# Down projections by Strassen's method on quarters, and one shared ring of buffers, in a two-layer encoder trunk

## The chip, the core and the metric

The kernel runs on one core of one Trainium2 chip. The metric is device time in microseconds (us) of one execution. A core has a matrix engine (PE, with its weight loads shown apart as PEld), a vector engine (DVE), an activation engine (ACT), a general engine (POOL) and queues for transfers (SP's above all). Each engine works off its own instructions strictly in their order, and engines wait for one another at semaphores.

## The reference

Two layers of a Conformer-like block on 512 tokens of width 1024, all in float32:

```python
for l in range(DEPTH):
    x = x + 0.5 * swiglu(rms_norm(x, ffn1_norm[l]), ffn1_w_gate[l], ffn1_w_up[l], ffn1_w_down[l])
    h = rms_norm(x, mix_norm[l])
    p = h @ w_in[l]
    attn = mla_group(p[..., :o_kv], p[..., o_kv:o_pe], p[..., o_pe:o_cv], ...)
    conv = conv_group(p[..., o_cv:], conv_w[l], conv_b[l], conv_ln_g[l], conv_ln_b[l])
    x = x + jnp.concatenate([attn, conv], axis=-1) @ w_out[l]
    x = x + 0.5 * swiglu(rms_norm(x, ffn2_norm[l]), ffn2_w_gate[l], ffn2_w_up[l], ffn2_w_down[l])
    x = rms_norm(x, post_norm[l])

def swiglu(x, w_gate, w_up, w_down):
    return (jax.nn.silu(x @ w_gate) * (x @ w_up)) @ w_down
```

The feed-forward width is 2816. `mla_group` is attention with 8 heads, `conv_group` a causal depthwise convolution with 31 taps over 512 channels, then a layer norm and a silu.

## The kernel before

**Layout.** x is held transposed: 8 tiles of 128 features by 512 tokens. Every float32 product is made as three matmuls of a shorter float type: weights and activations are split into a high part `hi` (a cast on ACT) and a low part `lo` (source minus high part, on DVE), and `mm3` adds hi\*hi, hi\*lo and lo\*hi in PSUM. So each weight tile that comes in by a transfer costs a cast on ACT and a subtraction on DVE before PE may use it (`load_w`, `split_into`).

**A feed-forward half** (`ffn_body`; four in all) goes through 11 pairs of 128-wide column blocks in chunks of 2, 3, 3 and 3 pairs. Pairs of the first chunk make gate and up plainly while DVE and ACT prepare the operands `X` (`operands`). A later pair (`pair`) makes gate and up by Strassen's method in Winograd's form on quarters: four quarters a11, a12, a21, a22 of the weights come in, three sums of them and s3 are made on DVE, and seven products of 24 matmuls with 256 columns go into the PSUM banks bx, by and bz. After a chunk, each of the 8 output tiles m is a plain down projection: a weight tile is loaded and split, 6 x 3 matmuls of 512 columns run, and DVE adds the result into x (`order["evicted"]`).

**A mixing stage** (`mix_body`; two) makes the joint projection, latent queries and keys, then the attention of 8 heads as a software pipeline over stages (`turn`, `scores`, `turn_p`, `values`, `turn_out`; the last PE step of a head pair is the transposition in `turn_out`). The convolution runs beside it on other engines. Of its four tiles of channels, kind "D" runs on DVE; kind "A" (c = 1 and 2) makes each of 30 taps as a product `pr` on ACT (L765) and an addition into `y` on POOL (L769). Then POOL sums the four tiles (L783 to L785), PE makes their mean (L787), a layer norm follows, and the output projection uses the attention's four tiles first and the convolution's four afterwards.

**What sets the order.** The program is written in one order; a scheduler with a model of times then lists each engine's instructions. Tiles come from pools. A pool gives its buffers out in the order in which the program asks, and a tile that finds none free waits for an earlier one's last reader. `slot()` is such a pool, the ring: 41 tiles of 128 x 512. `tmp()` is another, of 5. `pr` has three buffers of its own, `y` two, `acc` two, `R` two.

## Time and profile before

| what | us |
|---|---|
| median of 3 runs (lowest, highest) | 1832.68 (1830.99, 1833.28) |
| the profiled execution's own time | 1831.62 |
| its span, first to last instruction | 1829.9 |
| PE busy | 1812.2 |
| DVE busy | 1357.7 |
| ACT busy | 938.6 |
| POOL busy | 333.2 |

Lines of the profile name the place (L769 is line 769 of the kernel), the engine, the operation, the tiles written and read with their numbers left out (`y<-y,pr`), and a shape. In the page's row of slices each digit is the busy share, in tenths, of one fortieth of the span. In a timeline a row has its start, its length, and in brackets the idle time of the engine before it with what ended that. Consecutive instructions of one engine overlap a little, so a row's length is more than the distance to the next start.

### The profile page before, as it was taken

What the parts mean: (1) busy time and instruction counts of PE and PEld (TensorE: products, weight loads), DVE (VectorE), ACT (ScalarE), POOL (GpSimd) and SP (SyncE); (2) the same over time, 40 slices, a digit from 0 to 9 for tenths busy, and PEclk for the clock granted to TensorE, in tenths of its full rate; (3) what the DMA queues carried; (4) which work ended last, traced back from release to release, by engine and by line L of the source; (5) the groups of instructions that cost most, each with busy time, mean ns of one, the idle gap of its engine ahead of it and who ended that gap; (6) DMA issues with size and microseconds to landing.
All of it is one profiled execution on the core that took longest, in us unless ns stands there. A gap on an engine that the chain in (4) does not pass through costs nothing.

```text
span 1829.9 us, 28080 instructions
## 1 busy us (share of the span) xinstructions
PE 1812.2 (99%) x11334; PEld 1625.6 (89%) x11334; DVE 1357.7 (74%) x1775; ACT 938.6 (51%) x1477; POOL 333.2 (18%) x239
## 2 busy tenths in 40 slices
PE   9999999999999999999999999999999999999998
PEld 7898989888788898989888999998878788989897
DVE  7976767589956985858769677675999669767674
ACT  5553535457953453535734535354679435535354
POOL 1000000248943000000310000002589410000001
PEclk9999999999999999999999999999999999999999
DMA  6242422324123142423512414123250322424122
GB/s 225 72 136 62 143 65 81 116 75 138 36 81 98 47 139 65 141 67 96 170 52 64 153 56 152 55 88 116 78 134 19 109 82 64 144 64 137 61 84 78
DMA packets 55426, 175.73 MB, mean 96 GB/s; under 512 B 6272, under 2 KB 6656, under 8 KB 55296
## 3 DMA queue, kind: packets, MB, share of 16 engines
q1 hardware_dynamic: 54000, 169.74, 29.4%
q0 software_dynamic: 1152, 4.19, 1.3%
q8 instruction: 88, 1.44, 0.3%
q14 instruction: 42, 0.34, 0.1%
q10 hardware_dynamic: 144, 0.00, 0.0%
HBM read 171.82 MB, written 2.10 MB: 95 GB/s over the span
## 4 chain that ended last, share of the span: by engine, by line
PE 85%; DVE 5%; ACT 4%; POOL 2%; issue 2%; DMA 1%; SPq 0%; ACTq 0%; POOLq 0%; DVEq 0%
PE ps L148 27%; PE ps L150 27%; PE ps L149 27%; PE ps L707 1%; ACT pr L765 1%; POOL y L769 1%; ACT r L679 1%; DVE wl L141 1%; DVE t L309 1%; DVE r L304 1%; PE ps L673 1%; PE ps L694 1%; DVE cv L761 1%; ACT wh L135 1%; PE ps L191 0%
## 5 line engine op out<-in xcount | busy, mean ns | idle before, releaser
L149 PE MATMUL ps<-r,wh 128*128 128x256 f32 (+1 forms) x3292 | 1060.8, 324 | 0.0
L150 PE MATMUL ps<-r,wl 128*128 128x256 f32 (+1 forms) x3292 | 1053.7, 324 | 2.7 <-DVE wl L141 1.4
L148 PE MATMUL ps<-r,wh 128*128 128x256 f32 (+1 forms) x3292 | 1053.6, 326 | 0.5 <-ACT r L154 0.3
L149 PEld LDWEIGHTS ps<-r,wh 128*128 128x128 f32 x3292 | 626.5, 190 | 51.5 <-issue 2.4
L148 PEld LDWEIGHTS ps<-r,wh 128*128 128x128 f32 x3292 | 622.3, 190 | 56.0 <-ACT wh L135 1.5
L150 PEld LDWEIGHTS ps<-r,wl 128*128 128x128 f32 x3292 | 622.9, 190 | 54.7 <-DVE wl L141 3.9
L237 ACT CAST wh<-fr 128x1024 fp32r<-128x1024 f32 x216 | 226.9, 1051 | 314.0 <-PE ps L149 227.9
L135 ACT CAST wh<-raw 128x768 fp32r<-128x768 f32 (+3 forms) x212 | 185.3, 880 | 331.1 <-PE ps L149 156.3
L239 DVE TENSOR_TENSOR wl<-fr,wh 128x1024 fp32r<-128x1024 f32 x216 | 264.2, 1223 | 75.7 <-ACT wh L237 72.7
L184 POOL TENSOR_TENSOR acc<-acc,t 128x512 f32<-128x512 f32 x45 | 77.8, 1738 | 1292.6 <-ACT t L180 1291.8
L141 DVE TENSOR_TENSOR wl<-raw,wh 128x768 fp32r<-128x768 f32 (+3 forms) x196 | 205.7, 1055 | 120.3 <-ACT wh L135 118.8
L433 DVE SCALAR_TENSOR_TENSOR x<-ps,x 128x512 f32<-128x512 f32 x126 | 86.8, 689 | 113.3 <-PE ps L150 113.3
L769 POOL TENSOR_TENSOR y<-y,pr 128x511 f32<-128x511 f32 (+14 forms) x120 | 157.0, 1309 | 54.0 <-ACT pr L765 46.5
L765 ACT ACTIVATE pr<-r,vec 128x511 f32<-128x511 f32 (+14 forms) x120 | 85.0, 729 | 12.7 <-POOL y L769 12.7
L761 DVE SCALAR_TENSOR_TENSOR cv<-r,vec,cv 128x511 f32<-128x511 f32 (+14 forms) x120 | 87.8, 732 | 3.4 <-ACT cv L757 2.1
L154 ACT CAST r<-t 128x512 fp32r<-128x512 f32 x96 | 55.8, 620 | 35.1 <-DVE t L282 22.2
L155 DVE TENSOR_TENSOR r<-t,r 128x512 fp32r<-128x512 f32 x96 | 64.8, 687 | 10.2 <-ACT r L154 10.2
L237 ACT CAST wh<-raw 128x1024 fp32r<-128x1024 f32 x36 | 37.7, 1048 | 66.7 <-PE ps L149 66.7
L239 DVE TENSOR_TENSOR wl<-raw,wh 128x1024 fp32r<-128x1024 f32 x36 | 44.1, 1226 | 28.4 <-ACT wh L237 28.3
L357 DVE TENSOR_TENSOR raw<-fr,fr 128x1024 f32<-128x1024 f32 x36 | 44.0, 1223 | 15.6 <-DMA fr<-in_wgu 15.6
L148 PE MATMUL ps<-wh,r 128*128 128x288 f32 (+2 forms) x144 | 48.5, 337 | 0.8 <-ACT r L652 0.8
L673 PE MATMUL ps<-r,r 96*128 96x384 f32 (+3 forms) x128 | 45.0, 462 | 2.6 <-ACT r L679 2.4
(189 smaller groups left out, 1627.2 us busy)
## 6 DMA issues: line engine op xcount, KB each, us to landing
fr<-in_wgu SPq DMA_DIRECT2D x144, 512.0 KB, 3.6
raw<-in_wd SPq DMA_DIRECT2D x96, 384.0 KB, 3.2
raw<-in_wgu SPq DMA_DIRECT2D x30, 512.0 KB, 3.6
raw<-in_wd SPq DMA_DIRECT2D x32, 256.0 KB, 2.7
raw<-in_wcv SPq DMA_DIRECT2D x16, 512.0 KB, 3.6
raw<-in_wout SPq DMA_DIRECT2D x16, 512.0 KB, 3.6
wl<-in_wout POOLq DMA_DIRECT2D x8, 512.0 KB, 6.9
raw<-in_wql SPq DMA_DIRECT2D x6, 512.0 KB, 3.6
```

The source lines that it names most:

```text
L135: order["cast"] = A.copy(hi[:, :w], raw[:, :w]).ins
L141: (G if kind in POOLW.split() else V).tensor_tensor(lo[:, :w], raw[:, :w], hi[:, :w].bitcast(FP), ALU.subtract)
L148: T.matmul(o, lh, rh, start=first, stop=False, skip_group_check=free)
L149: T.matmul(o, lh, rl, start=False, stop=False, skip_group_check=free)
L150: return T.matmul(o, ll, rh, start=False, stop=last, skip_group_check=free).ins
L184: (eng or (V if last else G)).tensor_tensor(self.acc, self.acc, sq, ALU.add)
L237: A.copy(hi[:, :w], src[:, :w])
L239: V.tensor_tensor(lo[:, :w], src[:, :w], hi[:, :w].bitcast(FP), ALU.subtract)
L433: order["evicted"] = V.scalar_tensor_tensor(x[:, m, :], pd, 0.5, x[:, m, :], ALU.mult, ALU.add).ins
L761: V.scalar_tensor_tensor(acc[:, s:], u[c][:, :S - s], tap(k), acc[:, s:], ALU.mult, ALU.add)
L765: A.activation(pr[:, s:], u[c][:, :S - s], AF.Copy, scale=tap(k))
L769: order["conv"] = G.tensor_tensor(acc[:, s:], acc[:, s:], pr[:, s:], ALU.add).ins
```

## The change

1. The down projections of chunks of three pairs (all but the last chunk of the last feed-forward half: eleven) go by Strassen's method too: `down` makes, for each half g of the output tiles, seven products of 18 matmuls with 256 columns from quarters of the down weights, and adds them into x from the banks px, py and pz after each product. px is not started anew between its products b11, t2, t1 and b22. `pair` makes the operands for it: combinations u and v of its two results s and s2, each split.
2. Two of a pair's seven low parts (a12 and a22) are made by `summed`: ACT writes the negated cast, and a transfer issued on POOL adds the source from memory onto it. Low parts have five buffers.
3. The ring has 49 tiles and now also serves `acc`, `R`, the latent keys `ck`, the accumulators `y` and the products `pr`. `tmp` has 6. The operands' even and odd halves use the quarters' buffers `fr`.
4. In the first feed-forward half the norm's first sums stand after half of a plain product more, and a pair's silu steps are written earlier.

```diff
-RING = 41
+RING = 49
+LOS = 5
...
-    tmps = ctx.enter_context(tc.tile_pool(name="tmps", bufs=5))
+    tmps = ctx.enter_context(tc.tile_pool(name="tmps", bufs=6))
-    rpool = ctx.enter_context(tc.tile_pool(name="rp", bufs=2))
...
+        def summed(p, q, src):
+            lo = low()
+            A.activation(lo, src, AF.Copy, scale=-1.0)
+            G.dma_start(out=lo, in_=wgu[l, p, q], accum_op=ALU.add)
+            hi = wpool.tile([P, WC], FR, tag="wh", name=nm("wh"))
+            A.copy(hi, src)
+            return hi, lo
...
-            product(by, split_into("a12", a12), "b21", True, True)
+            product(by, summed(p, 1, a12), "b21", True, True)
...
-            product(bz, split_into("a22", a22), "t4", False, True)
+            product(bz, summed(p, 3, a22), "t4", False, True)
...
-            return [split(s), split(s2)]
+            if not quartered:
+                return [split(s), split(s2)]
+            h0, h1 = slice(0, HS), slice(HS, S)
+            b = slot(FR)
+            A.copy(b[:, h0], s[:, h0])
+            V.tensor_tensor(b[:, h1], s[:, h0], b[:, h0].bitcast(FP), ALU.subtract)
+            b2 = split(s2)
+            u, v = tmp(), tmp()
+            V.tensor_tensor(u[:, h0], s[:, h1], s2[:, h1], ALU.subtract)
+            V.tensor_tensor(u[:, h1], u[:, h0], s[:, h0], ALU.subtract)
+            V.tensor_tensor(v[:, h0], s[:, h0], s[:, h1], ALU.subtract)
+            V.tensor_tensor(v[:, h1], s2[:, h0], u[:, h1], ALU.add)
+            us, vs = split(u), split(v)
...
+        def down(act, chunk):
+            n = 2 * NP * P
+            for g in range(2):
+                a11, a12, a21, a22 = (quarter() for _ in range(4))
+                for q, t in enumerate((a11, a12, a21, a22)):
+                    nc.sync.dma_start(out=t[:, :n], in_=wdq[l, g, chunk, q])
+                s3 = wpool.tile([P, WC], FP, tag="raw", name=nm("raw"), bufs=3)
+                px, py, pz = bank(), bank(), bank()
...
+                times(px, a11, "b11", True)
+                add(0, 0, px, 1)
+                times(py, a12, "b21", True)
+                add(0, 0, py, 1)
+                for o, u, v in ((s3, a11, a21), (a21, a21, a22), (a11, a11, a21), (a12, a12, a11)):
+                    V.tensor_tensor(o[:, :n], u[:, :n], v[:, :n], ALU.add)
+                times(px, a11, "t2", False)
+                add(1, 0, px, -1)
+                times(pz, s3, "t3", True)
+                add(1, 1, pz, 1)
+                times(px, a21, "t1", False)
+                add(1, 1, px, -1)
+                times(pz, a22, "t4", False)
+                add(1, 0, pz, 1)
...
+                times(px, a12, "b22", False)
+                add(0, 1, px, 1)
...
+            if p0 and not last:
+                down(act, (p0 - CHUNKS[0][1]) // NP)
+                continue
...
-                pr = kpool.tile([P, S], FP, tag="pr", name=nm("pr"), bufs=3)
+                pr = slot()
```

`times` splits the quarter (`split_into`) and issues the 18 matmuls; `add` is one DVE instruction that adds a bank, halved and signed, into two tiles of x.

**Where instructions moved.** The changed file is longer, so its lines have other numbers: the attention's exponentials are L679 before and L756 now, the casts L154 and L159, the convolution's products L765 and L842, its additions L769 and L846, the mean L787 and L864, low parts L239 and L244, additions into x L433 and L431.

ACT in the first layer's attention, before (`pr` products between the exponentials):

```order
L679 ACTIVATE r756_4489,sums753_4486<-ps751_4484,mx754_4487 128x384
L679 ACTIVATE r757_4490,sums753_4486<-ps752_4485,mx754_4487 128x512
L652 ACTIVATE r759_4512<-ps758_4507,gqs729_4409 96x512
L765 ACTIVATE pr946_5186<-r605_3766,vec_78 128x484
L679 ACTIVATE r766_4525,sums753_4486<-ps762_4521,mx765_4524 128x128
L765 ACTIVATE pr947_5189<-r605_3766,vec_78 128x483
L679 ACTIVATE r767_4526,sums753_4486<-ps763_4522,mx765_4524 128x384
L679 ACTIVATE r755_4488,sums753_4486<-ps750_4483,mx754_4487 128x256
```

and now, where its first convolution products stand (r987 is the cast of the last head pair's transposed output, r637 the accumulator of c = 1, r1002 and later the products):

```order
L774 COPY r977_5565<-ps976_5564 128x512
L159 CAST r982_5592<-ps981_5587 128x512
L159 CAST r987_5615<-ps986_5610 128x512
L834 ACTIVATE r637_4128<-r688_4338,vec_75 128x512
L842 ACTIVATE r1002_5681<-r688_4338,vec_75 128x511
L842 ACTIVATE r1003_5684<-r688_4338,vec_75 128x510
L842 ACTIVATE r1004_5687<-r688_4338,vec_75 128x509
```

All 60 products of the layer moved from among the attention's instructions to behind its last cast; the second layer is the same.

POOL in the same mixing stage, before (`rtok` is the norm's root, `acc` the sum of squares of the query latents, `y556` the accumulator of c = 1):

```order
L166 TENSOR_TENSOR rtok582_3651<-vtok580_3644,minus_half_98 128x4
L769 TENSOR_TENSOR y556_3558<-y556_3558,pr919_5105 128x511
L769 TENSOR_TENSOR y556_3558<-y556_3558,pr920_5108 128x510
L769 TENSOR_TENSOR y556_3558<-y556_3558,pr921_5111 128x509
L769 TENSOR_TENSOR y556_3558<-y556_3558,pr922_5114 128x508
L769 TENSOR_TENSOR y556_3558<-y556_3558,pr923_5117 128x507
L184 TENSOR_TENSOR acc616_3834<-acc616_3834,t619_3840 128x512
```

and now, the first additions, behind the four transfers for the output projection's weights:

```order
L141 DMA wl991_5623<-in_wout 128x1024
L141 DMA wl994_5630<-in_wout 128x1024
L141 DMA wl997_5637<-in_wout 128x1024
L141 DMA wl1000_5644<-in_wout 128x1024
L846 TENSOR_TENSOR r637_4128<-r637_4128,r1002_5681 128x511
L846 TENSOR_TENSOR r637_4128<-r637_4128,r1003_5684 128x510
L846 TENSOR_TENSOR r637_4128<-r637_4128,r1004_5687 128x509
```

Fifteen additions stood ahead of the keys' roots before, and the others among the transfers; now all 60 stand behind the transfers, and each reads a product from the ACT rows above.

DVE in the first down stage, before (around the 2nd and 3rd of the eight output tiles, `wl` being a low part):

```order
L433 SCALAR_TENSOR_TENSOR x_76<-ps254_1473,x_76 128x512
L141 TENSOR_TENSOR wl273_1582<-raw271_1578,wh272_1580 128x768
L433 SCALAR_TENSOR_TENSOR x_76<-ps258_1499,x_76 128x512
L141 TENSOR_TENSOR wl277_1608<-raw275_1604,wh276_1606 128x768
L357 TENSOR_TENSOR raw286_1663<-fr282_1655,fr284_1659 128x1024
```

and now (ps270 is px, ps271 py, ps272 pz; t259 is the last pair's u and r262 its low part, t260 is v; raw291 and fr289 are sums of the second half's quarters):

```order
L402 TENSOR_TENSOR t259_1475<-t242_1312,t253_1435 128x256
L404 TENSOR_TENSOR t260_1476<-t242_1312 128x256
L431 SCALAR_TENSOR_TENSOR x_73<-ps271_1499,x_73 128x2x256
L244 TENSOR_TENSOR wl284_1622<-fr268_1492,wh283_1620 128x768
L403 TENSOR_TENSOR t259_1475<-t259_1475,t242_1312 128x256
L437 TENSOR_TENSOR raw291_1674<-fr287_1666,fr289_1668 128x768
L405 TENSOR_TENSOR t260_1476<-t253_1435,t259_1475 128x256
L160 TENSOR_TENSOR r262_1482<-t259_1475,r261_1481 128x512
L160 TENSOR_TENSOR r264_1486<-t260_1476,r263_1485 128x512
L437 TENSOR_TENSOR fr289_1668<-fr289_1668,fr290_1669 128x768
L431 SCALAR_TENSOR_TENSOR x_73<-ps270_1498,x_73 128x2x256
L431 SCALAR_TENSOR_TENSOR x_73<-ps272_1500,x_73 128x2x256
```

The last pair's combinations and splits now stand between the first additions into x of the down stage, and PE's first t2 matmuls of that pair need r261 and r262. PE's own order has 12 matmuls of t3 and 12 of t2, those of the other two pairs, ahead of them.

More of the change, by code (lines that the diff above doesn't have):

```diff
@@ L214, in spread_sb @@
         ps = spread(r)
[L215 removed]
+        R = slot()
         A.copy(R, ps)
@@ L310, in diff @@
                 return t
-            for n in ("b11", "b21"):
-                for i in range(2):
-                    X[n].append(halved((es if n == "b11" else od)[i][:, :, 0:HS]))
+            for i in range(2):
+                e, o = wide(quarter()), wide(quarter())
+                for j in range(2):
+                    for par, t in ((0, e), (1, o)):
+                        m = 4 * i + 2 * j + par
+                        V.scalar_tensor_tensor(t[:, j], x[:, m, :], gain[:, m:m + 1], R, ALU.mult, ALU.mult)
+                        yield
+                b11, b12, b21, b22 = (v[:, :, h * HS:(h + 1) * HS] for v in (e, o) for h in range(2))
+                for n, src in (("b11", b11), ("b21", b21)):
+                    X[n].append(halved(src))
                     yield
-            for i in range(2):
-                b11, b12, b21, b22 = (v[i][:, :, h * HS:(h + 1) * HS] for v in (es, od) for h in range(2))
                 t3 = diff(b12, b22)
@@ new lines, in pair @@
+            V.tensor_tensor(b[:, h1], s[:, h0], b[:, h0].bitcast(FP), ALU.subtract)
[6 more added lines that the diff above has]
+            us, vs = split(u), split(v)
+            return [{"b11": (b[:, h0], b[:, h1]), "b21": [w[:, h0] for w in b2], "b22": [w[:, h1] for w in b2],
+                     "t3": [w[:, h0] for w in us], "t2": [w[:, h1] for w in us],
+                     "t1": [w[:, h0] for w in vs], "t4": [w[:, h1] for w in vs]}]
@@ L392, in ffn_body @@
             act = []
+            last = p1 == NF // 2 and halved < KD
             for p in range(p0, p1):
@@ L435, in ffn_body @@
                     done(m)
-            if last and halved < KD:
+            if last:
                 ms = range(halved, KD)
@@ L893, in encoder_kernel @@
     w0 = [tuple(wpool.tile([P, WC], t, tag=tag, name=nm(tag), bufs=n)
-                for t, tag, n in ((FP, "raw", 3), (FR, "wh", 4), (FR, "wl", 4))) for _ in range(2)]
+                for t, tag, n in ((FP, "raw", 3), (FR, "wh", 4), (FR, "wl", LOS))) for _ in range(2)]
     def half_w(q, gu):
```

103 lines of the change are left out of this document (61 added, 42 removed).

## Prediction

> **What bounds the kernel now.** I read the page first: the busy shares, the slices and the chain that ended last.
>
> ```profile
> PE 1812.2 (99%) x11334; PEld 1625.6 (89%) x11334; DVE 1357.7 (74%) x1775; ACT 938.6 (51%) x1477; POOL 333.2 (18%) x239
> PE   9999999999999999999999999999999999999998
> POOL 1000000248943000000310000002589410000001
> PE 85%; DVE 5%; ACT 4%; POOL 2%; issue 2%; DMA 1%; SPq 0%; ACTq 0%; POOLq 0%; DVEq 0%
> ```
>
> PE is never idle for long and makes up 85% of the chain: 1829.9 us is the sum of its matmuls. POOL works in earnest twice, in the two mixing stages. Next I asked for busy time by stage: one gate/up pair, one stage of eight down projections, one layer's attention, and what follows the attention (columns: stage, length, then busy time of PE, PEld, DVE, ACT, POOL).
>
> ```profile
> 268.94:289.13 20.19, 20.19 (x170) 20.16 (x169) 16.57 (x18) 11.56 (x16) 0.00 (x0) 1.00 0.34 105
> 329.40:362.20 32.80, 32.80 (x146) 27.19 (x145) 22.10 (x26) 16.69 (x24) 10.17 (x6) 1.00 0.41 128
> 451.50:516.50 65.00, 61.87 (x440) 50.78 (x439) 55.70 (x104) 58.13 (x133) 59.17 (x49) 1.00 0.23 51
> 516.50:530.40 13.90, 13.77 (x62) 10.44 (x60) 8.30 (x14) 6.38 (x11) 1.03 (x1) 1.00 0.00 0
> ```
>
> The FFN stages are PE alone. Attention keeps four engines near full at once, POOL at 59 of 65 us: it works off the convolution's additions beside the attention.
>
> **The products.** Busy times of matmuls overlap, so I take distances between starts from the timeline, six matmuls apart in each form.
>
> ```profile
> 299.79 0.28 PE L150 MATMUL ps<-r,wl 128*128 128x256 f32 x1
> 300.51 0.28 PE L150 MATMUL ps<-r,wl 128*128 128x256 f32 x1
> 327.80 0.39 PE L150 MATMUL ps<-r,wl 128*128 128x512 f32 x1
> 329.16 0.39 PE L150 MATMUL ps<-r,wl 128*128 128x512 f32 x1
> ```
>
> 0.120 us for 256 columns, 0.227 for 512: the half-width matmul costs 6% more per column. A chunk of three pairs had 8 x 6 x 3 = 144 of the wide form, 32.6 us; now it has 2 x 7 x 3 x 2 x 3 = 252 of the narrow one, 30.2 us. The eighth that Strassen's method saves shrinks to 2.4 us, and eleven chunks give **-26.4 us**.
>
> **What DVE gets in the chunk.** Prices, again by starts: 0.60 for an addition of 512 columns into x, 0.865 for a low part of 768, 0.34 for 256 columns, 1.13 for 1024.
>
> ```profile
> 337.63 0.69 DVE L433 SCALAR_TENSOR_TENSOR x<-ps,x 128x512 f32<-128x512 f32 x1
> 338.23 1.82 DVE L141 TENSOR_TENSOR wl<-raw,wh 128x768 fp32r<-128x768 f32 x2
> 339.96 1.79 DVE L161 SCALAR_TENSOR_TENSOR r<-x,vec,r 128x512 fp32r<-128x512 f32 x1
> 277.51 0.42 DVE L376 TENSOR_TENSOR t<-t,t 128x256 f32<-128x256 f32 x1
> 277.85 1.22 DVE L359 TENSOR_TENSOR fr<-fr,fr 128x1024 f32<-128x1024 f32 x1
> 278.98 1.22 DVE L239 TENSOR_TENSOR wl<-fr,wh 128x1024 fp32r<-128x1024 f32 x1
> ```
>
> In a pair two low parts leave DVE (-2.3) and four combinations, two splits and a narrower split come (+2.3): 16.6 of 20.2 us as before. In the down stage DVE had 8 x 0.865 + 8 x 0.60 = 11.7 us of its own; now it has 14 x 0.865 + 8 x 0.865 + 14 x 0.60 = 27.4 us against 30.2 of PE, and each sum in px is read by DVE before PE may continue in it, with one product of 18 x 0.12 = 2.16 us for cover. I walked DVE's queue from the end of the last pair's b22 product (time 0). PE has 10 matmuls of b11, 18 of b21, 12 each of t3 and t2 until 6.2, then needs the last pair's u split. Before that split DVE has a product of 256, the first addition (its sum is ready at 1.3), a low part, two combinations, the addition of b21, a low part, a combination, a sum of quarters and another combination: the split ends near 7.1, so PE waits 0.8. t1 waits for the addition of t2, behind a split and a sum of quarters: about 0.9. In the second half t1 waits about 0.4 in the same way. I take 2.0 per stage, **+22 us**; the bounds are 0 (DVE's 27.4 is below 30.2) and twice that, since the next pair's six instructions of 1.13 stand in the same queue.
>
> The two low parts made by a subtracting transfer cost ACT a copy each and POOL an issue each; POOL is idle there. One such transfer is in the trace:
>
> ```profile
> wl<-in_wout POOLq DMA_DIRECT2D x8, 512.0 KB, 6.9
> L138 ACT ACTIVATE wl<-raw 128x1024 fp32r<-128x1024 f32 x4 | 4.2, 1050 | 0.0
> L139 POOL DMA_DIRECT2D wl<-in_wout x8 | 7.5, 936 | 0.5 <-ACT wl L138 0.5
> ```
>
> The buffer of a12's low part comes free after the t3 product of the pair before. From there to its use are t1, t4, b22, a11 (4 x 2.88 = 11.5 us); it needs a copy behind t3 (a row of 0.58 for that size stands below), the negation of 1.05, the issue of 0.94 and 6.9 us, 9.5 together. Cost 0, with 2.0 us to spare; a transfer that lands later than that stops PE by the rest. In the first FFN half of a product now stands ahead of the first sums, which hides this wait: **-1.4**.
>
> ```profile
> 24.60 1.05 PE L191 MATMUL ps<-ones,acc 128*128 128x1 f32 x8 [1.42 <-DVE acc L184]
> ```
>
> The shared ring's first user is the mixing stage. Before, products `pr` had three buffers of their own, and both engines' orders show them between the attention's work. Now `pr` is a ring slot, asked for after all of the attention's slots; in the new order all 60 ACT products of a layer stand behind the attention's last cast, and all 60 POOL additions behind them. PE's order is unchanged: last turn of the attention, then the mean of the convolution (L787, now L864), and only behind it the output projection. What these took:
>
> ```profile
> 392.28 7.18 POOL L769 TENSOR_TENSOR y<-y,pr 128x511 f32<-128x511 f32 x5 [21.08 <-ACT pr L765]
> 476.34 35.47 POOL L769 TENSOR_TENSOR y<-y,pr 128x508 f32<-128x508 f32 x27 [1.12 <-ACT pr L765]
> 511.76 1.27 POOL L783 TENSOR_TENSOR t<-r,y 128x512 f32<-128x512 f32 x1
> 513.11 1.27 POOL L784 TENSOR_TENSOR t<-t,y 128x512 f32<-128x512 f32 x1
> 514.46 1.26 POOL L785 TENSOR_TENSOR t<-t,r 128x512 f32<-128x512 f32 x1
> 516.02 0.66 PE L725 MATMUL ps<-cst,t 128*128 128x128 f32 x4 [0.78 <-DVE t L714]
> 516.51 1.02 PE L787 MATMUL ps<-t,onesm 128*128 128x512 f32 x2
> 516.71 0.58 ACT L154 CAST r<-ps 128x512 fp32r<-128x512 f32 x1 [3.04 <-PE ps L725]
> 458.76 0.63 ACT cv L757
> L765 ACT ACTIVATE pr<-r,vec 128x511 f32<-128x511 f32 (+14 forms) x120 | 85.0, 729 | 12.7 <-POOL y L769 12.7
> ```
>
> Before, POOL was done at 515.7 and the mean ran at 516.51, without a wait. Now the cast ends at 517.3, the accumulator's start 0.63 and the first product 0.7 later, 518.6. ACT then makes products faster (0.7) than POOL adds them: 35.47 / 27 = 1.314 each. 60 x 1.314 = 78.8, the three sums 3 x 1.35 = 4.0, so the mean can start at 601.4 instead of 516.5: 84.9 us in which PE's queue stands. The chain behind it (14 us until the convolution's rows of the projection) has the same order and moves rigidly. From this goes what the attention gains without the products on ACT: PE is idle 65.00 - 61.87 = 3.1 us in it, so 0 to 3.1, and I take 1.5 since other ACT work stays. Two layers: **+167 us** (bounds: 1.27 each, the busy time of the sums, -5 in all; 7.18 / 5 = 1.436, the early stretch's rate, +15).
>
> The early rate has two splits of weights beside it on DVE, and they were slowed too, 2.07 us for the 768 columns that cost 0.865 above:
>
> ```profile
> 394.16 1.41 DVE L141 TENSOR_TENSOR wl<-raw,wh 128x576 fp32r<-128x576 f32 x1
> 398.20 2.07 DVE L141 TENSOR_TENSOR wl<-raw,wh 128x768 fp32r<-128x768 f32 x1
> ```
>
> I take the rate of the 27, since after the attention DVE has nothing to split. The Trainium skill (SBUF — State Buffer, "SBUF: two separate sides") says that a DVE instruction with two SBUF inputs and a GpSimd one that reads SBUF hold one port pair exclusively. By that rule the additions, now beside an idle DVE, go at the lower rate; without it the early rate would stand, and the two layers would cost 182.
>
> A long stand of PE has no row: its longest wait is the 1.42 above, and the granted clock is 1.00 in every stage quoted. I price the restart at 0 to 3 us per layer, since PE's 13.77 of 13.90 us has little slack, and take 0. The Trainium skill (TensorE: Matmul & The Clock Gate, Part 1) has the array at half rate for about 3.4 us after an idle window; by that the sum would be some 3 us higher, and no run here shows it yet.
>
> **Sum.** The profiled execution took 1831.62 us (span 1829.9), 1.1 below the median of 1832.68. 1831.6 - 26.4 + 22 - 1.4 + 167 = **1993 us**.
>
> **Rivals.** *Faster after all*: the additions run beside the attention again, as POOL's row of slices shows for the old order. Then the sum is 1831.6 - 26.4 - 1.4 plus the down stages' 0 to 22: 1804 to 1826. It decides at a stand of PE below (27.8 - 22) / 2 = 2.9 us per layer, or 13.9 without waits in the down stages. Against it: both queues are worked off in order, and the casts wait for PE. 0.04, of which 0.01 lands within 0.2%.
>
> *The transfers land late*: 72 of them (two in each of 36 pairs) have 2.0 us to spare. If POOL's issue beside a fuller DVE makes them land after 12 us instead of 6.9, each costs 3.1 us past its cover, 223 together: 2216. For it: the trace has them only in a stage where nothing waited closely. Against: DMA is busy 0.34 in a pair, and each pair adds 1 MB to 2. 0.06.
>
> *DVE bounds the down stages*: 27.4 own plus 6.8 for the next pair, 34.2 against 30.2, 4 us per stage: 2015, within the range. 0.15.
>
> *The output projection's first half fills the stand*: four groups of 12 wide matmuls, 10.9 us, need nothing from the convolution. Put ahead of the mean they would hide part of a stand, but the work behind it would lack them: 1970 to 1985. The order has them behind. 0.05.
>
> The forecast itself has 0.70. A difference below about 0.2% (3.7 us) can't be told from none here. Faster 0.03, same 0.01, slower 0.96. The range starts at 1993 - 22 (no waits in the down stages) - 5 (additions at 1.27) - 3 (the attention's full gain) = 1963, and ends at 1993 + 22 + 15 (the early rate) + 6 (slow restarts) = 2036; I give 1958 to 2035. It leaves out the late transfers and the faster case, and a little more.
>
> **What would show it.** Two stands of PE of about 83 us, each ended by POOL at the mean (L864), near zero in PE's row of slices from about 515 to 598 and from about 1502 to 1586; 60 POOL additions in one unbroken stretch of some 79 us behind the attention; the 7 x 18 narrow products at 0.120 each; small waits of PE for DVE's additions to x (L431) and splits in the down stages, about 2 us each. Wrong if the POOL additions start before the last turn, if PE waits for `wl<-in_wgu` transfers, or if a down stage takes above 35 us.

## The result, and the profile after

The changed kernel took 2097.0 us, median of four runs (2095.6 to 2102.8), against 1832.8 (1831.0 to 1833.3): a ratio of 1.145, 95% interval 1.1426 to 1.1473. Slower, as forecast, but by 264 us where 160 were expected; 2097 lies above the range of 1958 to 2035. The profiled execution took 2096.15 us (span 2094.0).

Its page: the busy time of the engines, then PE, POOL and the granted clock (PEclk, the share of its full speed at which PE was let run) in 40 slices of 52 us.

```profile
PE 1830.5 (87%) x12522; PEld 1691.7 (81%) x12522; DVE 1509.3 (72%) x2121; ACT 1089.7 (52%) x1689; POOL 379.2 (18%) x311
PE   9989899999319998989999998999993199999899
POOL 1000000240584000000130000002406840000001
PEclk9999999999659999999999999999996599999999
```

The two stands are there, with POOL's additions in them and the clock falling while PE stands. PE's waits (us in all, times, longest) show a second loss that the forecast did not have:

```profile
PE ps L864 <- POOL t L862: 161.2, 2, 80.6
PE ps L153 <- ACT e L349: 26.0, 30, 1.1
PE ps L153 <- ACT r L159: 20.2, 13, 2.0
PE ps L154 <- DVE r L160: 16.7, 12, 1.7
PE ps L153 <- DVE x L431: 16.4, 14, 2.3
PE ps L196 <- DVE r L189: 5.1, 2, 3.0
```

Next to the 161.2 us of the two stands there are 79.3 us of waits of about 1 us each (2.3 at most) in the pairs and quartered down stages: the second to fifth line. One chunk of three pairs with its down stage (from wait to wait) now, and a stretch of one chunk's length of before:

```profile
150.22:252.70 102.48, 94.57 (x758) 92.68 (x757) 80.63 (x106) 53.86 (x74) 5.18 (x6) 0.98 0.48 124
231.40:324.80 93.40, 93.40 (x649) 87.53 (x648) 65.05 (x73) 41.40 (x56) 0.00 (x0) 1.00 0.24 74
```

9.1 us more per chunk, where the forecast had 0.4 less (2.4 saved, 2.0 waited): eleven times the difference is 104 us, as much as was missed in all, if the one chunk is taken for all eleven. Less three pairs of 21.49 us (a row further down) it leaves 38 us for the down stage, above the 35 that the prediction named as a sign of being wrong.

What such a wait does besides standing is seen at the first quartered down stage. PE's rows (start, duration, what ended the idle time before):

```profile
150.22 0.28 PE L155 MATMUL ps<-r,wl 128*128 128x256 f32 x1
152.42 0.51 PE L153 MATMUL ps<-r,wh 128*128 128x256 f32 x2 [1.92 <-ACT r L159]
154.36 0.44 PE L154 MATMUL ps<-r,wh 128*128 128x256 f32 x1 [1.44 <-DVE r L160]
...
155.02 0.41 PE L154 MATMUL ps<-r,wh 128*128 128x256 f32 x1
155.23 0.41 PE L155 MATMUL ps<-r,wl 128*128 128x256 f32 x1
```

After the second wait the matmuls start every 0.21 us instead of 0.12. Two windows in a row there, and below them the same at two other places (columns: us, then busy time of PE, PEld, DVE, ACT, POOL, then the granted clock):

```profile
151.14:154.55 3.41, 0.70 (x3) 0.49 (x4) 2.63 (x6) 1.24 (x2) 0.00 (x0) 1.00 0.55 194
154.55:157.97 3.42, 3.42 (x16) 3.24 (x16) 3.21 (x5) 1.66 (x2) 0.00 (x0) 0.50 0.00 0
...
274.00:277.41 3.41, 1.60 (x14) 1.43 (x13) 2.41 (x4) 2.69 (x3) 0.00 (x0) 1.00 0.42 153
277.41:280.83 3.42, 3.42 (x19) 3.42 (x18) 3.17 (x5) 0.30 (x2) 0.86 (x1) 0.50 0.37 34
...
376.42:379.84 3.42, 1.77 (x16) 1.60 (x15) 3.42 (x6) 1.04 (x1) 0.57 (x1) 1.00 0.00 1
379.84:383.25 3.41, 3.41 (x29) 3.32 (x28) 3.14 (x5) 1.05 (x1) 0.00 (x0) 1.00 0.16 42
```

The granted clock changes in steps of 3.41 us: each stretch at half clock in this trace, from its first 40 us to the second stand, lasts 3.41 us or a whole number of times that. Here a window with PE busy for 0.70 or 1.60 us is followed by one at half clock, one with 1.77 is not (the last section has windows of other runs, where the border lies elsewhere). So waits that together take more than about half of a window can cost some 1.5 us more in the next: 16 matmuls with 0.095 each.

For the account I took the start-to-start distances of all matmuls of L153 to L155 and their counterparts: the products at their usual spacing (0.120 us for 256 columns, 0.2275 for 512); what distances exceed it by over 0.25 us each (waits); the excess of matmuls in windows at half clock; and everything else (attention, sums, the stands). Counted so, a wait is some 0.2 us longer than PE's idle time in the list above. From the first matmul's start to the last, in us:

| kernel | products | waits | half clock | else | sum |
|---|---|---|---|---|---|
| before | 1610.7 | 12.4 | 0 | 200.2 | 1823.3 |
| after | 1583.0 | 111.7 | 23.4 | 369.3 | 2087.4 |
| t3_after | 1583.0 | 89.8 | 24.6 | 368.0 | 2065.4 |
| conv_spread | 1583.0 | 106.7 | 25.6 | 261.6 | 1976.9 |
| chain | 1583.0 | 64.5 | 6.7 | 368.4 | 2022.6 |
| no_sum | 1583.0 | 59.5 | 7.8 | 366.2 | 2016.5 |
| plain_down | 1610.7 | 14.2 | 4.1 | 361.3 | 1990.3 |
| best_d | 1583.0 | 33.1 | 5.9 | 262.9 | 1884.9 |
| d_plain | 1610.7 | 8.4 | 2.4 | 260.4 | 1881.9 |
| plain_g | 1610.7 | 7.1 | 2.0 | 211.9 | 1831.7 |

From before to after: -27.7 products, +99.3 waits, +23.4 half clock, +169.1 else, of which 161.2 are the stands. The other rows are experiments, told next.

### The profile page after: what moved, and what is told of

Its sections match the earlier page's. It is cut to its first block, busy times and chain, and to the rows that moved or that the text cites. A ratio compares the mean times of both kernels' runs of the same rounds, so it can differ in the third digit from the quotient of the medians.

```text
span 2094.0 us, 31408 instructions
## 1 busy us (share of the span) xinstructions
PE 1830.5 (87%) x12522; PEld 1691.7 (81%) x12522; DVE 1509.3 (72%) x2121; ACT 1089.7 (52%) x1689; POOL 379.2 (18%) x311
## 5 line engine op out<-in xcount | busy, mean ns | idle before, releaser
L153 PE MATMUL ps<-r,wh 128*128 128x256 f32 (+1 forms) x3688 | 1124.4, 310 | 64.0 <-ACT e L349 26.0
L154 PE MATMUL ps<-r,wh 128*128 128x256 f32 (+1 forms) x3688 | 1128.1, 308 | 17.0 <-DVE r L160 16.7
L155 PE MATMUL ps<-r,wl 128*128 128x256 f32 (+1 forms) x3688 | 1113.0, 307 | 4.8 <-DVE wl L143 3.5
L153 PEld LDWEIGHTS ps<-r,wh 128*128 128x128 f32 x3688 | 710.6, 194 | 109.0 <-ACT e L349 32.0
L154 PEld LDWEIGHTS ps<-r,wh 128*128 128x128 f32 x3688 | 716.2, 194 | 52.8 <-DVE r L160 20.1
L155 PEld LDWEIGHTS ps<-r,wl 128*128 128x128 f32 x3688 | 708.9, 194 | 37.5 <-DVE wl L143 4.8
L242 ACT CAST wh<-fr 128x1024 fp32r<-128x1024 f32 (+1 forms) x276 | 259.7, 946 | 300.9 <-PE ps L154 172.0
L244 DVE TENSOR_TENSOR wl<-fr,wh 128x1024 fp32r<-128x1024 f32 (+1 forms) x276 | 299.2, 1093 | 11.5 <-ACT wh L242 10.4
L137 ACT CAST wh<-raw 128x1024 fp32r<-128x1024 f32 (+4 forms) x124 | 111.0, 907 | 215.8 <-PE ps L154 115.4
L846 POOL TENSOR_TENSOR r<-r,r 128x495 f32<-128x495 f32 (+22 forms) x120 | 145.1, 1231 | 126.3 <-ACT r L842 122.1
L143 DVE TENSOR_TENSOR wl<-raw,wh 128x1024 fp32r<-128x1024 f32 (+4 forms) x108 | 116.1, 1080 | 65.3 <-ACT wh L137 64.8
L864 PE MATMUL ps<-t,onesm 128*128 128x512 f32 x4 | 4.1, 1138 | 161.2 <-POOL t L862 161.2
L159 ACT CAST r<-t 128x512 fp32r<-128x512 f32 x129 | 77.6, 618 | 106.9 <-DVE t L403 36.0
L864 PEld LDWEIGHTS ps<-t,onesm 128*128 128x128 f32 x4 | 1.0, 313 | 161.7 <-POOL t L862 161.7
L431 DVE SCALAR_TENSOR_TENSOR x<-ps,x 128x512 f32<-128x512 f32 x154 | 104.5, 685 | 28.9 <-PE ps L155 28.6
L189 POOL TENSOR_TENSOR r<-r,t 128x512 f32<-128x512 f32 x45 | 75.2, 1679 | 236.7 <-ACT t L185 129.4
L358 ACT CAST wh<-fr 128x1024 fp32r<-128x1024 f32 x72 | 75.7, 1051 | 30.9 <-PE ps L154 30.7
L838 DVE SCALAR_TENSOR_TENSOR cv<-r,vec,cv 128x511 f32<-128x511 f32 (+14 forms) x120 | 87.6, 730 | 2.9 <-ACT cv L834 1.7
```

The source lines that it names most:

```text
L137: order["cast"] = A.copy(hi[:, :w], raw[:, :w]).ins
L143: (G if kind in POOLW.split() else V).tensor_tensor(lo[:, :w], raw[:, :w], hi[:, :w].bitcast(FP), ALU.subtract)
L153: T.matmul(o, lh, rh, start=first, stop=False, skip_group_check=free)
L154: T.matmul(o, lh, rl, start=False, stop=False, skip_group_check=free)
L155: return T.matmul(o, ll, rh, start=False, stop=last, skip_group_check=free).ins
L159: A.copy(hi, src)
```

## The experiments

My theory was that the stand comes from the ring, and the rest from the order in which DVE, ACT and PE work in pairs and quartered down stages. Ratios are to the kernel before, on the same chip. The scheduler lists the instructions anew for each, so that an edit in one place can move others.

**plain_down: the down products as before.**

```diff
-                    act += pair(p, p0 > 0 and not last)
-            if p0 and not last:
-                down(act, (p0 - CHUNKS[0][1]) // NP)
-                continue
+                    act += pair(p, False)
```

> The eleven chunks take their down products plainly again (144 matmuls of 512 in place of 252 of 256, no sums of quarters, no combined activations); the transfers of the low parts and the shared ring stay. Theory: the 104 us that the forecast missed lie at the quartered down stages and in the pairs' order that they bring; a chunk of pairs and down falls from 102.5 to about 94 us: 1990 to 2005. Rival (they lie in pairs because of the subtracting transfers, and the quartered down gains its 2 us each): 2080 to 2125.

1998.2 us (1.0904, 1.0888 to 1.0920). A chunk takes 93.40 us again, without a wait:

```profile
226.90:320.30 93.40, 93.40 (x649) 87.47 (x649) 58.43 (x68) 46.89 (x62) 5.18 (x6) 1.00 0.48 120
```

So the quartered down products, in this kernel, cost 99 us in place of the 4.4 that the forecast saw saved. And the transfers, which stay here, cost next to nothing beside plain down products: 1998.2 is 1832.2 + 161.2 and 5 us.

**t3_after: PE's order in the pairs.** Before, PE had 10 matmuls of t3 ahead of t2 and 14 between t2 and t1 (1.7 us, while ACT copies t2's result out of bx, which t1 adds to). In the changed kernel's steady state it has 20 and 4: 0.5 us.

```diff
-            product(bz, split_into("s3", s3), "t3", True, True)
+            w3 = split_into("s3", s3)
+            with tc.issue_after(order["last"]):
+                product(bz, w3, "t3", True, True)
```

> Only PE's order changes: the 24 matmuls of t3 stand wholly between t2 and t1 (20 stood ahead of t2 and 4 behind it). Theory: t1's wait for ACT's copy of t2's result (PE L153 for ACT L349, 26.0 us in 30 waits) goes, since 2.9 us of matmuls now cover a copy that ends some 1.7 us after t2; 2066 to 2074. Rival (the copy is late because ACT is late, whatever PE does): the waits move ahead of t2 or t4 and the time stays at 2093 to 2101.

2071.8 us (1.1302, 1.1283 to 1.1320), 25 less, as the theory has it. The 26.0 us of waits for the copy `e` are gone; 9.2 us in ten waits came in their place (L153 for ACT's L349, tile `t`). These stand ahead of t2 and are for the copy of b11's result out of bx: with t3 moved away, only b21 is left to cover that copy. Waits in the down stages fell a little.

**chain: DVE's order in the down stages.** The rows quoted with the change show a sum of the second half's quarters (raw291) between the steps that make u and v. In the trace that sum stands for a transfer:

```profile
151.30 0.42 DVE L403 TENSOR_TENSOR t<-t,t 128x256 f32<-128x256 f32 x1
152.41 0.96 DVE L437 TENSOR_TENSOR raw<-fr,fr 128x768 f32<-128x768 f32 x1 [0.69 <-DMA fr<-in_wdq]
153.28 0.42 DVE L405 TENSOR_TENSOR t<-t,t 128x256 f32<-128x256 f32 x1
153.62 0.68 DVE L160 TENSOR_TENSOR r<-t,r 128x512 fp32r<-128x512 f32 x1
```

```diff
-                        hi, lo = split_into(name, src, n)
+                    with tc.issue_after(order["acts"]) if g == 0 and name in ("t1", "t4") else nullcontext():
+                        hi, lo = split_into(name, src, n)
...
+                with tc.issue_after(order["acts"]) if g else nullcontext():
                     for o, u, v in ((s3, a11, a21), (a21, a21, a22), ...
...
+            with tc.issue_after(added[10]) if added else nullcontext():
                 V.tensor_tensor(s3, a11, a21, ALU.add)
```

(`order["acts"]` is the low part of v, `added[10]` the addition of the second half's t3.)

> Only the order is changed, on DVE: of a quartered down stage, the combinations u and v of the activations and their low parts go ahead of the second half's sums (L437) and of two weight splits, and the next pair's first sum (L369) goes behind most of the down stage's additions into x. Theory: PE's waits in down stages (ACT L159 20.2 us, DVE L160 16.7, DVE L431 16.4: 53 us) come from work that DVE has in its queue ahead, some of it standing for a transfer; most of them go, and with them the stretches of half TensorE clock behind them (some 23 us): 2022 to 2052. Rival (DVE is the bound of the down stage, and only the place of the wait moves): 2085 to 2100.

2029.7 us (1.1077, 1.1061 to 1.1094): 67 us less by another order, without an instruction less on DVE. Of the three waits of 53.3 us, 9.2 are left, and the windows at half clock fall from 23.4 us to 6.7:

```profile
PE ps L153 <- DVE x L436: 5.3, 2, 2.7
PE ps L154 <- DVE r L160: 2.4, 11, 0.2
PE ps L153 <- ACT r L159: 1.5, 7, 0.3
```

The rival, DVE as the bound, falls. Not all of the 67 us is the down stages: PE's waits for the copy `e` in the pairs fell too, from 26.0 to 10.3 us, since the scheduler gave PE another order there.

**no_sum: low parts by DVE again.**

```diff
-            product(by, summed(p, 1, a12), "b21", True, True)
+            product(by, split_into("a12", a12), "b21", True, True)
-            product(bz, summed(p, 3, a22), "t4", False, True)
+            product(bz, split_into("a22", a22), "t4", False, True)
```

> The two low parts of each pair are made by DVE again (72 subtractions of 1.09 us), without the transfers; the quartered down stages and the shared ring stay. Theory: PE's order becomes 13 matmuls of t3 ahead of t2 and 11 behind it, so t1's wait for ACT's copy shrinks by 0.84 us per pair, and DVE has the room: 2072 to 2088. Rival (DVE, now at 19 of 20.2 us in a pair, is late for weights): 2100 to 2130.

2028.3 us (1.1071, 1.1051 to 1.1091): 69 less, far below both expectations. DVE got 72 more subtractions and PE waited less for it. One thing that went are DVE's own waits for quarters, of after and then of no_sum:

```profile
DVE raw L369 <- DMA fr<-in_wgu: 51.2, 31, 3.7
DVE fr L370 <- DMA fr<-in_wgu: 45.9, 22, 3.3
DVE raw L437 <- DMA fr<-in_wdq: 31.3, 22, 3.9
DVE fr L437 <- DMA fr<-in_wdq: 16.1, 10, 2.4
```

```profile
DVE raw L437 <- DMA fr<-in_wdq: 3.1, 3, 1.5
DVE raw L369 <- DMA fr<-in_wgu: 2.8, 6, 0.8
DVE fr L437 <- DMA fr<-in_wdq: 0.2, 1, 0.2
```

With the transfers DVE stands 144.5 us for quarters, without them 6.1. That alone does not make PE stand: in plain_down DVE still stood 87.6 us for quarters and PE for nothing in the chunk above, and chain, 67 us faster than the changed kernel, still had 104.0. The scheduler's order changed too: u's and v's four combinations now follow one another, ahead of the sum of quarters that stood among them, much as chain has it, and PE's waits for the copy `e` fell from 26.0 to 6.1 us. The next run tries to part the two.

**dma_only and fr6: why DVE stands.**

```diff
+            A.copy(spare[:, 0:8], a12[:, 0:8])
+            G.dma_start(out=spare, in_=wgu[l, p, 1], accum_op=ALU.add)
...
```

(The same follows for a22.)

> As no_sum (low parts by DVE), with the 72 transfers brought back as a load alone: into a spare tile that nobody reads, each started by a copy of 8 columns on ACT when its quarter has landed; one low-part buffer (5 to 4) makes the room. PE's and DVE's orders are those of no_sum. Theory B (the transfers' traffic slows the quarters' own loads, and DVE stands for them): DVE's waits for quarters rise from 6 to over 80 us and the time from 2028 to 2060 to 2100. Theory A (not the traffic, but the order of the engines and how long the transfers' quarters are held): waits under 40 us, 2020 to 2040.

2059.0 us (1.1241, 1.1218 to 1.1264), 31 above no_sum; DVE's waits for quarters are 72.3 us. Both theories had a part, and neither range holds it: with no_sum's orders the transfers bring back half of DVE's waits and at most 31 of the 69 us. At least 38 go with the rest: the orders, and 72 negated casts less on ACT. How much of the 31 is traffic is not shown. A low-part buffer less is in it, and the small copies, for which ACT itself stands 124.6 us for transfers and which hold a quarter until they are done. The quarters' loads took 4.0 us to land (median) instead of 3.4:

```profile
DVE raw L374 <- DMA fr<-in_wgu: 36.3, 14, 3.7
DVE fr L375 <- DMA fr<-in_wgu: 32.5, 18, 3.1
fr<-in_wgu SPq DMA_DIRECT2D x144, 512.0 KB, 4.0
```

One more buffer for quarters (`bufs=6`, paid with two temporaries) was to show the holding of buffers:

> One more buffer for the quarters (5 to 6), paid with two temporaries (6 to 4). Without the transfers DVE's waits for quarters fell from 144.5 us to 6.1 and the time by 69. Theory A (the transfers' source quarters are held longer, so five buffers are too few): DVE waits for quarters under 60 us, time 2040 to 2075. Theory B (the transfers slow the quarters' own loads, or four temporaries are too few): DVE still waits over 120 us, time 2085 to 2110.

2103.3 us (1.1472, 1.1455 to 1.1489). DVE's waits for quarters fell to 58.9 us, as theory A has it, and the time did not: PE now waited 31.1 us for the transfers' own landing (`wl<-in_wgu`). That time is in theory B's range, the wait in theory A's. Four temporaries may have done it; the run settles nothing about the rest of the 69 us.

**filler: is it the idle time that halves the clock?**

```diff
+                        if name == "t2" and g == 0 and k == NP - 1:
+                            idle = psum.tile([P, S], FP, tag="cv", ...)
+                            with tc.issue_after(order["last"]):
+                                for _ in range(16): T.matmul(idle[:, 0:HS], hi[:, 0:P], ...)
```

> Sixteen matmuls of 256 into a spare bank, whose result nobody reads, stand in PE's order just ahead of the matmul that waits for the cast of u in each of the eleven quartered down stages (16 x 0.12 = 1.9 us in a wait of some 1.9 us); nothing else moves. Theory (a 3.4 us stretch at half TensorE clock follows a stretch of 3.4 us in which PE stood for some 1.9 us or more): most of the thirteen short stretches at half clock go and the products there run at 0.12 again: 2074 to 2085. Rival (the clock falls whatever PE does there, or the waits are longer than the filler): 2093 to 2105.

2089.5 us (1.1403, 1.1386 to 1.1420), between the two ranges: 7.5 less with 176 matmuls more. The fillers only took the place of the waits for the cast (20.2 us before, 0.3 now; eleven fillers of 2.1 us are 23), so that what was gained is the clock's. The half-clock excess fell from 23.4 to 15.4 us and stretches at half clock outside the two stands and the first 40 us went from fifteen to nine. At the place of the first rows above PE is now busy for 2.16 us where it was for 0.70, and the next window keeps its clock:

```profile
150.70:154.10 3.40, 2.16 (x17) 1.86 (x15) 2.81 (x5) 1.16 (x2) 0.00 (x0) 1.00 0.64 207
154.10:157.50 3.40, 2.53 (x19) 2.33 (x20) 3.32 (x6) 1.65 (x3) 0.00 (x0) 1.00 0.00 0
```

That PE's idle time halves the clock is borne out; the gain is smaller than expected, with nine stretches left and other waits grown (for additions into x from 16.4 to 21.7 us).

**own_pr, own_both, conv_spread: what makes the stand.**

```diff
-                pr = slot()
+                pr = kpool.tile([P, S], FP, tag="pr", name=nm("pr"), bufs=3)
```

> The conv's products get three buffers of their own again; the room comes from one low-part buffer (5 to 4) and one temporary (6 to 5), the ring keeps its 49. Theory (the stand of PE is the shared ring alone): the two waits of L864 for the conv's additions, 80.6 us each, go; 2097 - 161 = 1936, with 5 us either way for the smaller pools; the chunks of pairs and down products keep their 102 to 103 us. Rival (the additions, once early, slow attention): 1945 to 1960. Rival (the stand has another cause, the additions themselves being later than before): over 2050.

2087.7 us (1.1391, 1.1374 to 1.1408): the stands stay, 83.5 us each. ACT now makes the first products early, at 418.95 us, so they are not what POOL waits for. The profile puts the wait of its first addition down to the attention's last low part, which ends together with L834:

```profile
418.95 1.34 ACT L842 ACTIVATE pr<-r,vec 128x511 f32<-128x511 f32 x2 [2.25 <-DVE r L548]
POOL r L846 <- DVE r L160: 108.3, 2, 54.2
541.63 1.52 ACT L834 ACTIVATE r<-r,vec 128x512 f32<-128x512 f32 x2
```

L834 starts the two accumulators, ring slots as well, and does it behind the attention's last cast. So they were given their own too (`ys` in `kpool`, two buffers; products two; for the room four low parts and four temporaries).

> The conv's two accumulators get buffers of their own as well as its products (two each; paid with one low-part buffer and two temporaries, the ring keeps its 49). With the products alone out of the ring, POOL's first addition still waited for the attention's last low part, because the accumulator's slot came free only then. Theory (either of the two in the ring is enough to hold the conv back): both stands of 80 to 84 us go, 2088 - 161 = 1920 to 1945. Rival (a third tile, or the order of POOL, holds it): 2060 to 2095.

2054.5 us (1.1212, 1.1194 to 1.1231). The stands are gone, 161.2 us down to 6.8, and the time fell by only 33, since the subtracting transfers now land too late for PE:

```profile
PE ps L155 <- DMA wl<-in_wgu: 87.0, 38, 4.3
PE ps L864 <- POOL t L862: 6.8, 2, 3.4
```

That is the rival "the transfers land late", at a price of 87 us of waits and more half clock; with the changed kernel's pools it did not occur. Which pool does it is open: own_pr, with four low parts and five temporaries, has 14.0 us of these waits, and fr6, with five and four, 31.1. Then the ring was left as it is, and only the conv's taps (with the loads of the output projection's weights) were written earlier in the program:

```diff
+                if step == "c1":
+                    advance(by_pool, 15)
...
         for step in range(H + 6):
+            advance(by_pool, 8)
+            advance(by_dve, 8)
             for stage, lag in STAGES:
```

> The changed kernel with its one ring and all its pool sizes; only the place in the program where the conv's taps are written moves: fifteen taps of the first POOL channel behind that channel's gate, the others eight per step of the attention's loop, instead of all behind that loop. Theory (the ring is large enough, but its slots go to whatever is written first, and attention stood first): POOL adds beside attention, the two stands of 80.6 us fall to between 0 and 12 us each: 1935 to 1960. Rival (the ring lacks the slots, and attention then waits for the conv): the stand moves into attention, over 2030.

1982.8 us (1.0813, 1.0795 to 1.0831), between the two: 114 us less with the same ring and pools, so the ring's size is not what made the stand, but who asks it first. By the table some 25 us per layer stay (261.6 against plain_g's 211.9). About half of it are two waits inside the attention in each layer, where ACT makes up to fifteen products in a row that three buffers used to hold back; the rest was not taken apart:

```profile
PE ps L762 <- ACT r L786: 15.0, 2, 7.5
PE ps L780 <- ACT r L759: 11.3, 2, 5.7
```

**Repairs together.** best_a joins conv_spread, no_sum, t3_after and chain; best_b adds a fifth buffer for high parts; best_d writes the taps in twos behind the exponentials; d_plain is best_d with plain down products.

> Quartered down products with all that helped alone: the conv's taps spread over attention, low parts by DVE, t3 between t2 and t1, DVE's order in the down stages. Theory (the waits that stay are some 30 us, against 27.7 of saved products): 1840 to 1865. Rival (nearly all waits go): 1812 to 1832. Rival (the order of DVE, with 72 more subtractions on it, brings the waits back): 1870 to 1900.

> As best_a, with a fifth buffer for high parts of weights in the room of the fifth for low parts. Theory (PE's waits for the cast of a weight's high part, 10 to 11 us, come from the four buffers): 10 to 15 us below best_a. Rival (they come from ACT's order): within 4 us of best_a, or above it where four low parts are too few.

> As best_b, with the conv's taps written in twos behind each of the attention's exponentials in place of eights per step, so that ACT no longer computes up to fifteen products in a row ahead of what attention waits for. Theory (the two layers' attention, 24 us longer than before each in best_b, comes back to within 5 to 10 us): 1845 to 1860. Rival (attention lacks ring slots, whatever ACT's order): 1875 to 1885. Rival (everything hidden): under 1833, and the quartered products pay.

> As best_d, but with the eleven chunks' down products taken plainly. Theory (the quartered products' 27.7 us saved are eaten by what is left of their waits, even with all repairs): within 8 us of best_d, either way. Rival (the quartered products pay once repaired): 15 to 28 us above best_d.

1894.6 (1.0332, 1.0316 to 1.0347), 1883.6 (1.0273, 1.0258 to 1.0288), 1894.5 (1.0339, 1.0322 to 1.0356) and 1891.4 us (1.0318, 1.0302 to 1.0333). best_a lies in its second rival's range, but not for that reason alone: 26 us of PE's waits are again the two inside the attention. best_b and d_plain came as their theories have it, best_d in none of its ranges. The fifth buffer halves the waits for a weight's cast (11.0 to 5.3 us) and gives 11 us. Twos in place of eights were no gain: the sum ahead of the mean now waits for a DVE channel, and PE 10.9 us for it in each layer. best_d and d_plain differ by 3 us: by the table 27.7 us of products saved against 24.7 more of waits and 3.5 more of half clock. Even with all these repairs the quartered down products are worth nothing here.

both_best, the repairs with own_both's tiles and the transfers, was to add up:

> The quartered kernel with all three repairs: conv tiles of its own, t3 between t2 and t1, DVE's order in the down stages. Theory (the repairs add up): 2030 - 161 - 10 = 1855 to 1870, so that the quartered products with their remaining waits still cost 20 to 40 us over the kernel before. Rival (with attention and pairs freed, the 26 us of saved products show): 1805 to 1832. Rival (smaller pools bring new waits): 1870 to 1895.

1972.5 us (1.0764, 1.0743 to 1.0785). It didn't, and lies above all three ranges: PE waits 66.2 us for the copies into temporaries ahead of t2. Four temporaries and t3_after's order, which leaves these copies less cover, are both in it, so the third rival is not shown apart. The last two leave the transfers out; plain_g has plain down products too, so that of the change only the ring and its pools are left.

> Quartered down products with low parts by DVE, DVE's repaired order in the down stages, and conv tiles of their own as in own_both (four low-part buffers, four temporaries). Theory: the conv hides as in the kernel before, the quartered products gain 2 to 3 us over plain ones at best, and four temporaries cost something: 1835 to 1860. Rival (attention as before and few waits): under 1829, faster than the kernel before. Rival (four temporaries choke the pairs, as copies into them waited 66 us in both_best): over 1875.

> As best_g with the down products taken plainly: of the change only the ring and its pool sizes are left. Theory: the kernel before within 6 us, 1828 to 1842; best_g within 15 us of it on either side. Rival (the ring and the smaller pools have a cost of their own): over 1850.

1898.3 (1.0361, 1.0344 to 1.0378) and 1841.7 us (1.0048, 1.0033 to 1.0063). plain_g closes the account: without the quartered products, the transfers and the conv's late start 8 of 264 us are left. That one came as its theory has it, but not "within 15 us" of best_g, which is 57 above: best_g has four temporaries against it again (22.3 us of waits for copies), 11.0 us of waits for weights' casts, and more half clock. No version here beats the kernel before.

## Why the prediction was wrong

- *The eighth saved, -26.4:* right. 27.7 us by the account.
- *The shared ring, +167:* right in size and in place: a stand of 80.6 us per layer for 84.9 priced, 83.4 with what the attention was to gain. The additions went at 56.68 / 46 = 1.23 each behind the attention, for 1.314 taken, as the rule of the Trainium skill that I weighed (SBUF — State Buffer, "SBUF: two separate sides") would have it beside an idle DVE. DVE was busy for 0.00 of these 56.68 us (the third busy time of the second row):

```profile
544.12 56.68 POOL L846 TENSOR_TENSOR r<-r,r 128x511 f32<-128x511 f32 x46 [61.04 <-ACT r L842]
544.12:600.80 56.68, 0.00 (x0) 0.00 (x0) 0.00 (x0) 37.25 (x61) 55.59 (x47) 0.50 0.00 0
```

  Its reason was half right: I named the products' slots; own_pr against own_both shows that the accumulators' slots are enough to hold the conv back (the products' alone were not tried), and conv_spread that it is the order of asking.
- *Waits of 2.0 us per down stage, +22:* the step that failed. I had u's low part ready 0.9 us after PE wants it (7.1 against 6.2). In the trace PE wants it at 150.34, which puts the end of b22 at 144.1, and the low part ends at 154.30: 10.2 us where I had 7.1. The silu of b22, with which the chain begins, stands on ACT behind a cast that waited for DVE and behind a weight's cast, and starts 2.2 us late; 0.69 more is the sum's wait for its quarter:

```profile
145.10 0.62 ACT L159 CAST r<-t 128x512 fp32r<-128x512 f32 x1 [0.83 <-DVE t L390]
145.62 0.83 ACT L242 CAST wh<-raw 128x768 fp32r<-128x768 f32 x1
146.36 0.37 ACT L392 ACTIVATE t<-ps 128x256 f32<-128x256 f32 x1
```

  I had walked one queue of two, and no transfer. The waits of this kind took 53.3 us instead of 22, in eleven stages, and chain, which changes this order, leaves 9.2 of them.
- *Pairs, no wait:* a step that was missing. DVE's load was worked out there and is as forecast, PE's order was not: four matmuls behind t2 where fourteen had been, 26.0 us. One pair with its wait, in the columns of the windows above:

```profile
111.56:133.05 21.49, 20.41 (x171) 20.21 (x169) 16.66 (x22) 14.11 (x21) 1.73 (x2) 1.00 0.55 133
```

- *PE's restart, 0 to 3 us per layer, and nothing elsewhere:* the price at the stands was small, but the rule was applied to long stands alone. The short waits halved the clock fifteen times; some 18 of the 23.4 us are matmuls of 256 columns, which never follow a stand. The Trainium skill (TensorE: Matmul & The Clock Gate, Part 1) has a free-running window of 3413 ns, and half rate after an idle one; the window is as it says, but here 1.6 us of work in it did not keep the clock (274.00 in the rows above).
- *The transfers, cost 0:* right beside plain down products (plain_down), wrong beside quartered ones, where removing them gave 69 us. They did not land late. At most 31 us go with the transfers themselves (dma_only), at least 38 with the orders that the scheduler then lists and the work that ACT is rid of; by which way the 31 come is not shown. I had asked only when a transfer lands.
- *First norm's sums, -1.4:* that wait is gone, but PE now stands 3.54 us right behind it, for the norm's next step, where the kernel before had no wait, and the clock is at half from 31.7 to 38.5 us. At the other end of the FFNs L196 waits 5.1 us for DVE's L189:

```profile
32.77 2.07 PE L215 MATMUL ps<-t,ones 128*128 128x512 f32 x2 [3.54 <-DVE t L211]
```

Together: of the 104 us, 31 are the waits of the down stages above the 22 forecast, 26 the pairs' waits and 23 the clock. The rest is mostly the 20 us by which the account's waits (99.3 more, from start to start) exceed the 79.3 of idle time; it was not taken apart.

Of the rivals, the faster case and the output projection ahead of the mean did not come. "The transfers land late" did not come in the changed kernel (`wl<-in_wgu` stops PE for 0.6 us in all) and came in own_both with smaller pools. "DVE bounds the down stages" falls with chain: 67 us went with the order, and DVE had no less to do.

## What to carry to other kernels

Walk every engine's queue that feeds a step, not the busiest one, and look at what stands between a result and its reader in each: four matmuls of cover where fourteen had been cost as much as the whole change was to save. When buffers are pooled, ask who asks first, and remember that each of several tiles can be the one that waits. Where a matrix engine is near its peak, price a wait by its length plus what the clock may take in the next window.

## What the runs showed of the hardware

The clock is granted by windows of 3.41 us. In the changed kernel it stayed full after windows with 1.77, 1.80 and 1.81 us of PE work, and the next one ran at half after 1.49 and 1.60, though no single wait in the pairs and down stages was longer than 2.3 us. The border is not the same everywhere. In conv_spread, below, it stayed full after 1.60 and fell after 1.77; in filler it once fell after 1.95 (from 1294.24). So these runs show that several short waits in one window can halve the clock, and not at which sum they do:

```profile
1845.10:1848.51 3.41, 1.60 (x14) 1.39 (x12) 2.92 (x6) 0.45 (x1) 0.00 (x0) 1.00 0.40 115
1848.51:1851.93 3.42, 1.77 (x12) 1.54 (x12) 3.14 (x5) 1.22 (x3) 0.00 (x0) 1.00 0.36 115
1851.93:1855.34 3.41, 2.66 (x13) 2.44 (x12) 3.38 (x6) 1.13 (x2) 0.00 (x0) 0.50 0.02 4
```

Beside 72 transfers of 512 KB that add onto a tile, two in a pair, the quarters' loads of the same size landed in 4.0 us (median, dma_only), and in 3.4 without them (no_sum). That is no fixed price: own_both has the same number of such transfers and 3.4, the kernel before has them in no pair and 3.6.
